# A two-layer diffusion trunk: fp32 products issued four by column group, norms spread by transposes, softmax sums by products with ones

## The chip, the cores and the metric

One core of a Trainium2 chip runs the whole program; the other cores are idle. The metric is the device time of one execution in microseconds (us), lower is better. The kernel before takes 1757.51 us, the median of three runs (1754.27 to 1760.52).

## What is computed

A trunk of two layers over 1024 latent tokens and 256 context tokens of width 1024, all in fp32. Cut to what the change touches:

```python
shift, scale, gate = jnp.split((silu_c @ ada_w[i] + ada_b[i])[:, None, :], 3, axis=-1)   # per layer, for c and c_ctx
a = modulate(rmsnorm(x, norm_g[i]), shift, scale)      # x * rsqrt(mean(x*x) + eps) * g * (1 + scale) + shift
...
# layer 0, latent attention: q, kv and the gate come out of a @ w_in
q = rmsnorm(cq, q_norm_g) @ w_uq;  kv = rmsnorm(ckv, kv_norm_g) @ w_ukv
p = jax.nn.softmax(s, axis=-1)                         # 1280 keys, 8 heads, 1024 queries
o = einsum('bhqk,bkhd->bqhd', p, v)
y = (o * silu(gate)) @ w_out
x = x + gate * y                                       # the adaLN gate
# layer 1, Hyena: two long convolutions; then the final rmsnorm
```

## The kernel before, in words

Tensors lie feature-major: 128 features on the partitions, tokens along the free axis, 512 at a time. Large products are made in three fp32r passes (`mm3`, lines 117 to 121): each operand is split into a rounded high part, copied by ScalarE (ACT, line 96), and the rest, a subtraction on VectorE (DVE, line 97). TensorE (PE) gets one 128x512 matmul for each pass. A scheduler in the tile framework sets each engine's order when the program is built; the code's order and the pools' buffers are what it starts from.

Four kinds of small product are made in plain fp32, and every one of them appears as two records in the trace, since such a matmul runs as two passes.

- **AdaLN** (`ada`, lines 133 to 162). silu(c) and silu(c_ctx) are two of 32 columns of a stationary tile `sc`. Each 512 columns of the weights give one matmul, 128x32 against 128x512, whose result lies on 32 of the 128 partitions of one bank: the group q (0 to 3) is chosen by `tile_position=(0, 32 * q)`. There are four calls: layer 0's shift and scale (four groups, pages of 512 columns, during the first 60 us), then, between the input projections of `work` (lines 570 to 584), layer 0's gate (two groups), layer 1's shift and scale (four) and layer 1's gate (two), out of two buffers `aw` of 1024 columns. Eight feature tiles make each; a matmul is issued as its columns have landed. All in all 96 matmuls.
- **Sums of squares** (`rms`, lines 345 to 375). ACT squares a tile (line 355), a matmul with a 128x32 tile of ones adds it over the partitions, again in column group k % 4 (line 356). Squares lie in three buffers of the pool `stage` in layer 0, in three of `sq` in layer 1's norm, in four at the end. Then the sums are transposed to columns (line 363), and DVE makes 1/rms of them. There are 12 such norms.
- **Spread** (`spread`, lines 377 to 383). The 1/rms column of 128 tokens, broadcast to 128 columns, is the stationary operand against the identity: an fp32 product that puts the row on every partition. Four of them fill a bank.
- **Softmax denominators** (`attend`, lines 773 to 830). The attention runs through 16 units (head, half of the queries) of 10 key tiles. For each key tile PE makes the scores S, ACT the exponentials p, DVE splits p and adds it to `acc` (line 804); PE multiplies by the values into O, two tiles later. Beside this the next unit's queries are multiplied by all keys once more for the row maxima (`row_max`, lines 724 to 739): two banks `apx`, each reduced by DVE (line 733). After a unit, in steps between the next unit's key tiles: O times the gate (line 816); four fp32 matmuls of 128 columns with ones, in the four column groups (line 821); a RECIPROCAL of 128x128 (line 823); four fp32 matmuls with `pick`, which spread the result to all partitions (line 828); and the multiplication (line 829). The bank for both comes from the pool `pj` of two, which also serves queries, keys and values.

The filters of layer 1 (`filters`, lines 268 to 342) are made in the first 440 us, interleaved with the input projections in a fixed ratio of generator steps: 120 filter steps to 60 of `work`. `ring` (line 201) is DVE work of such a step. SyncE (SP) issues nearly all loads, in one queue.

Of the kernel before, what the change touches and what calls it, by code (L numbers as in the profile page):

```python
# [11 lines left out]
F32 = mybir.dt.float32  # L12
F32R = mybir.dt.float32r
# [6 lines left out]
P = 128  # L20
# [26 lines left out]
def run(gen):  # L47
    """The value that a generator returns."""
    while True:
        try:  # L50
            next(gen)
        except StopIteration as e:
            return e.value


class Net:
# [42 lines left out]
    def feed(self, tiles, bufs=3, side=None):  # L99
        """The weights [128, K * 128] of the coming projections, in their order."""  # L100
# [4 lines left out]
    def weights(self):  # L105
        """The next piece of the weights, the one after it being loaded as well."""
# [26 lines left out]
    def ada(self, layer, part, page, bank, width=1024, queue=None):  # L133
        """part 0: shift and scale, part 1: gate."""
        nc = self.nc
        res, gs = self.adac[layer]
        ps = bank()
        nq = 2 if part else 4
        np_ = 32 * nq
        for k in range(KD):  # L140
            for s in range(0, nq * 512, width):
                w = page()
                o = 2048 * part + s
                (queue or nc.sync).dma_start(out=w, in_=self.a["adaw"][layer, k, :, o : o + width])
                for j in range(0, width, 512):
                    q = (s + j) // 512
                    nc.tensor.matmul(ps[32 * q : 32 * q + 32, :], lhsT=self.sc[:, k, :], rhs=w[:, j : j + 512],
                                     start=(k == 0), stop=(k == KD - 1), tile_position=(0, 32 * q))
            yield
        row = page()  # L150
        nc.scalar.copy(out=row[:np_, :512], in_=ps[:np_, :])
        tp = bank().rearrange("p (j c) -> p j c", j=4)
        for j in range(4):
            nc.tensor.transpose(out=tp[:, j, :np_], in_=row[:np_, j * P : (j + 1) * P], identity=self.ident[:np_, :np_])
        for r in range(2):
            c = slice(16 * part, 16 * part + 4 * nq)
            nc.vector.tensor_tensor(out=res[:, c, r].rearrange("p (q j) -> p j q", j=4), in0=tp[:, :, r:np_:32],
                                    in1=self.col(f"b{layer}", 16 * part, 4 * nq).rearrange("p (q j) -> p j q", j=4),
                                    op=ALU.add)
            if part == 0:  # L160
                nc.vector.scalar_tensor_tensor(out=gs[:, :, r], in0=res[:, 8:16, r], scalar=1.0,
                                               in1=self.col(f"g{layer}", 0, 8), op0=ALU.add, op1=ALU.mult)

# [37 lines left out]
    def ring(self, two, page, ze, zo, same):  # L201
        """Residues of 8-tile sequences ze (mod x^1024-1), zo (mod x^1024+1) in the 8 blocks."""
# [17 lines left out]
        B = [page().rearrange("p (s j c) -> p s j c", s=2, j=2) for _ in range(2)]  # [+-, j]  # L220
# [3 lines left out]
        t = page().rearrange("p (r s c) -> p r s c", r=2, s=2)  # [re/im, +-]  # L224
# [26 lines left out]
    def forward(self, two, bank, mats, i, b):  # L251
        """Spectrum of block i, [128, (re | im)] in one bank."""
# [92 lines left out]
    def rms(self, xs, n, bank, sqtile):  # L345
        """1/rms of n <= 512 tokens as columns [128, n / 128]."""
# [1056 lines left out]
```

## Time and profile before

| | |
|---|---|
| median of three runs | 1757.51 us |
| lowest, highest | 1754.27, 1760.52 us |
| span of the profiled execution, first to last instruction | 1753.2 us |
| mean granted TensorE clock | 0.995 |
| PE busy (matmul) | 1687.9 us, 96% |
| PE weight loads | 1310.8 us, 75% |
| DVE busy | 1408.3 us, 80% |
| ACT busy | 759.3 us, 43% |
| moved by DMA | 207.23 MB |

The span leaves out what lies before the first and after the last instruction; the profiled execution has no other time of its own, and its span stands 4.3 us under the median. Busy time is the union of an engine's instructions; matmuls overlap in the pipeline, so that the start-to-start distance is what one costs. A waiting time is put down to whoever released the waiting instruction last.

### The profile page before, as it was taken

Reading aid. Unit: us, or ns where it says so; the run is one execution under the profiler, and the core shown is the slowest. Engines: PE = TensorE matmul, PEld = TensorE weight load, DVE = VectorE, ACT = ScalarE, POOL = GpSimd, SP = SyncE. Lnnn points to the kernel's source line nnn. Section 1 sums busy time; section 2 is a strip of 40 time slices with the busy share of each in tenths; the row PEclk is TensorE's granted clock in tenths of the full one; section 3 lists DMA queues with packets and bytes.
Section 4 is the critical chain, followed back from the end, with each engine's and each line's share of the span. In section 5 each row is a group of like instructions: output and inputs, shape, how many; then the busy total and the mean of one; then the engine's idle time right before and its main releaser. Section 6 shows DMA issues by size and latency. Waiting matters only on the chain.

```text
span 1753.2 us, 23341 instructions
## 1 busy us (share of the span) xinstructions
PE 1687.9 (96%) x8368; PEld 1310.8 (75%) x8368; DVE 1408.3 (80%) x2528; ACT 759.3 (43%) x1315; POOL 15.1 (1%) x43
## 2 busy tenths in 40 slices
PE   7999999799999999999999999999999999999996
PEld 2367666687788888888877766888888888887874
DVE  4786978796687877887877455999999999999956
ACT  4533444435455555555555344433433343343313
POOL 1000000000000000000000010000000000000000
PEclk9999999999999999999999999999999999999999
DMA  9766666436101001010022772232332333234545
GB/s 308 249 186 193 193 199 204 138 93 194 36 27 43 19 29 40 19 32 25 19 67 79 245 249 87 84 101 88 106 114 81 104 87 111 91 118 128 188 149 209
DMA packets 139033, 207.23 MB, mean 118 GB/s; under 512 B 13386, under 2 KB 67361, under 8 KB 138788
## 3 DMA queue, kind: packets, MB, share of 16 engines
q1 hardware_dynamic: 135780, 195.05, 35.6%
q0 software_dynamic: 3136, 10.69, 1.9%
q8 instruction: 66, 1.08, 0.3%
q14 instruction: 51, 0.42, 0.1%
HBM read 149.97 MB, written 53.61 MB: 116 GB/s over the span
## 4 chain that ended last, share of the span: by engine, by line
PE 81%; DMA 9%; DVE 6%; ACT 2%; issue 1%; SPq 1%; DVEq 0%; ACTq 0%
PE pj L119 12%; PE pj L121 12%; PE pj L120 12%; PE apx L731 2%; PE S L119 2%; PE S L795 2%; PE S L120 2%; PE S L794 2%; PE S L121 2%; PE apx L732 2%; PE O L121 2%; PE O L120 2%; PE O L119 2%; PE fu L119 2%; DMA dec<-in_dec 2%; PE fy L119 2%
## 5 line engine op out<-in xcount | busy, mean ns | idle before, releaser
L96 ACT CAST w<-wr 128x512 fp32r<-128x512 f32 (+1 forms) x154 | 93.7, 609 | 276.0 <-PE pj L120 150.3
L119 PE MATMUL pj<-a,w 128*128 128x512 f32 x512 | 203.2, 397 | 1.7 <-ACT a L389 1.7
L120 PE MATMUL pj<-a,w 128*128 128x512 f32 x512 | 203.3, 397 | 0.0
L121 PE MATMUL pj<-a,w 128*128 128x512 f32 x512 | 203.1, 398 | 0.0
L797 ACT ACTIVATE p<-S 128x512 f32<-128x512 f32 x160 | 95.7, 598 | 167.6 <-PE S L795 160.7
L97 DVE TENSOR_TENSOR w<-wr,w 128x512 fp32r<-128x512 f32 (+1 forms) x154 | 102.0, 670 | 63.4 <-ACT w L96 63.0
L804 DVE TENSOR_TENSOR acc<-acc,p 128x512 f32<-128x512 f32 x144 | 99.1, 688 | 29.0 <-ACT p L797 28.6
L97 DVE TENSOR_TENSOR p<-p 128x512 fp32r<-128x512 f32 x160 | 109.7, 685 | 8.9 <-ACT p L96 8.6
L96 ACT CAST bh<-raw 128x512 fp32r<-128x512 f32 x128 | 77.1, 620 | 88.2 <-DVE raw L1043 70.3
L119 PEld LDWEIGHTS pj<-a,w 128*128 128x128 f32 x512 | 96.4, 188 | 22.9 <-ACT a L389 2.4
L120 PEld LDWEIGHTS pj<-a,w 128*128 128x128 f32 x512 | 96.5, 188 | 21.4 <-issue 1.7
L121 PEld LDWEIGHTS pj<-a,w 128*128 128x128 f32 x512 | 96.6, 189 | 18.5 <-DVE w L97 0.3
L733 DVE TENSOR_REDUCE cm<-apx 128x1 f32<-128x512 f32 (+1 forms) x192 | 108.3, 594 | 2.2 <-PE apx L732 1.5
L96 ACT CAST p<-p 128x512 fp32r<-128x512 f32 x160 | 99.4, 621 | 5.0
L121 PE MATMUL pj<-pg,w 128*128 128x512 f32 (+1 forms) x248 | 95.7, 387 | 4.2 <-DVE w L97 4.2
L119 PE MATMUL pj<-pg,w 128*128 128x512 f32 (+1 forms) x248 | 95.7, 387 | 0.6 <-ACT pg L389 0.5
L120 PE MATMUL pj<-pg,w 128*128 128x512 f32 (+1 forms) x248 | 96.3, 388 | 0.0
L97 DVE TENSOR_TENSOR bl<-raw,bh 128x512 fp32r<-128x512 f32 x128 | 84.5, 684 | 9.1 <-ACT bh L96 8.8
L119 PE MATMUL u<-bh,fm 128*128 128x256 f32 (+1 forms) x200 | 66.6, 334 | 11.1 <-ACT bh L96 10.7
L731 PE MATMUL apx<-kn,qn 128*128 128x512 f32 (+1 forms) x192 | 69.9, 369 | 2.9 <-DVE cm L733 2.8
L305 DVE TENSOR_TENSOR kk<-ph,dec 128x512 f32<-128x512 f32 x64 | 42.6, 684 | 32.9 <-DMA dec<-in_dec 20.0
L119 PE MATMUL fy<-bh,dm 128*128 128x256 f32 (+1 forms) x200 | 64.1, 320 | 2.4 <-ACT bh L96 2.4
(297 smaller groups left out, 4396.8 us busy)
## 6 DMA issues: line engine op xcount, KB each, us to landing
aw<-in_adaw SPq DMA_DIRECT2D x32, 512.0 KB, 5.0
kd<-ko SPq DMA_DIRECT2D x128, 128.0 KB, 2.0
wr<-in_hw SPq DMA_DIRECT2D x64, 256.0 KB, 2.6
kt<-kd SPq DMA_DIRECT2D x56, 256.0 KB, 2.7
wr<-in_w SPq DMA_DIRECT2D x34, 256.0 KB, 3.5
dec<-in_dec SPq DMA_DIRECT2D x64, 128.0 KB, 2.5
pg<-in_adaw SPq DMA_DIRECT2D x32, 256.0 KB, 6.1
wr<-in_wo SPq DMA_DIRECT2D x32, 256.0 KB, 3.2
```

Of the source, the lines that this page charges most:

```text
L96: self.nc.scalar.copy(out=hi, in_=raw)
L97: self.nc.vector.tensor_tensor(out=lo, in0=raw, in1=hi, op=ALU.subtract)
L119: mm(out, lhsT=w[0], rhs=x[0], start=start, stop=False)
L120: mm(out, lhsT=w[0], rhs=x[1], start=False, stop=False)
L121: mm(out, lhsT=w[1], rhs=x[0], start=False, stop=stop)
L305: nc.vector.tensor_tensor(out=kk, in0=ps, in1=dec.broadcast_to([P, 2, 2, P]), op=ALU.mult)
L731: mm(b[:, :w], lhsT=qn[0][:, c], rhs=kn[0][:, o : o + w], start=True, stop=False)
L732: mm(b[:, :w], lhsT=r1[:, c], rhs=krh[:, o : o + w], start=False, stop=True)
L733: v.tensor_reduce(out=cm[:, t, i : i + 1], in_=b[:, :w], axis=AX.X, op=ALU.max)
L794: mm(S, lhsT=krh[:, c], rhs=r1, start=False, stop=False)
L797: act.activation(out=p, in_=S, func=AF.Exp, scale=ASCALE)
L804: v.tensor_tensor(out=acc, in0=acc, in1=p, op=ALU.add)
```

## The change

1. `packed` issues up to four fp32 matmuls of different column groups directly one after the other, from the last group to the first; each is tied to the one before by `issue_after`. The first one issued is the one whose data come last.
2. `ada` takes a list of parts. Layer 0's shift and scale is as before, four groups in each feature tile; layer 1's shift and scale comes next; the gates of both layers are made together in one call of four groups. That is 24 groups of four in place of 96 matmuls issued apart, 16 of them after layer 0's shift and scale.
3. `rms` squares up to four tiles before it issues their group. In layer 0 the squares lie in the pool of 41 pages, in layer 1's norm in four buffers.
4. `spread` uses a transpose of the broadcast column in place of an fp32 product with the identity.
5. A unit's end: `acc` is split into high and low parts by ACT and DVE; two fp32r matmuls of 512 columns with a 128x128 tile of ones put the sum on every partition; the RECIPROCAL has 128x512 elements, and its result is multiplied out of SBUF. `pick` is gone. The work of line 816 is unchanged.

Nothing else changes but comments. The diff, cut:

```diff
+    def packed(self, mms):
+        nc = self.nc
+        def mm(out, w, x, start, stop, q):
+            return nc.tensor.matmul(out, lhsT=w, rhs=x, start=start, stop=stop, tile_position=(0, 32 * q))
+        prev = mm(*mms[-1], len(mms) - 1)
+        for q in range(len(mms) - 2, -1, -1):
+            with self.tc.issue_after(prev.ins), self.tc.high_priority():
+                prev = mm(*mms[q], q)
...
-    def ada(self, layer, part, page, bank, width=1024, queue=None):
+    def ada(self, parts, page, bank, width):
...
-            for s in range(0, nq * 512, width):
-                w = page()
-                o = 2048 * part + s
-                (queue or nc.sync).dma_start(out=w, in_=self.a["adaw"][layer, k, :, o : o + width])
-                for j in range(0, width, 512):
-                    q = (s + j) // 512
-                    nc.tensor.matmul(ps[32 * q : 32 * q + 32, :], lhsT=self.sc[:, k, :], rhs=w[:, j : j + 512],
-                                     start=(k == 0), stop=(k == KD - 1), tile_position=(0, 32 * q))
+            cols = []
+            for layer, first, n in parts:
+                for s in range(0, n * 512, width):
+                    wd = min(width, n * 512 - s)
+                    w = page(wd)
+                    o = 512 * first + s
+                    nc.sync.dma_start(out=w, in_=self.a["adaw"][layer, k, :, o : o + wd])
+                    cols += [w[:, j : j + 512] for j in range(0, wd, 512)]
+            self.packed([(ps[32 * q : 32 * q + 32, :], self.sc[:, k, :], w, k == 0, k == KD - 1)
+                         for q, w in enumerate(cols)])
...
-        for k, x in enumerate(xs):
-            q = k % 4
-            sq = sqtile()
-            nc.scalar.activation(out=sq[:, :n], in_=x, func=AF.Square)
-            nc.tensor.matmul(ss[32 * q : 32 * q + 32, :n], lhsT=self.ones, rhs=sq[:, :n], start=(k < 4),
-                             stop=(k + 4 >= nk), tile_position=(0, 32 * q))
+        for k0 in range(0, nk, 4):
+            group = []
+            for k in range(k0, min(k0 + 4, nk)):
+                sq = sqtile()
+                nc.scalar.activation(out=sq[:, :n], in_=xs[k], func=AF.Square)
+                q = k - k0
+                group.append((ss[32 * q : 32 * q + 32, :n], self.ones, sq[:, :n], k < 4, k + 4 >= nk))
+            self.packed(group)
...
-            self.nc.tensor.matmul(out[:, P * j : P * j + P], lhsT=r[:, j : j + 1].broadcast_to([P, P]),
-                                  rhs=self.ident, start=True, stop=True)
+            self.nc.tensor.transpose(out=out[:, P * j : P * j + P], in_=r[:, j : j + 1].broadcast_to([P, P]),
+                                     identity=self.ident)
...
-        for n, _ in enumerate(self.ada(0, 0, page, abank, 512, nc.sync)):
+        for n, _ in enumerate(self.ada([(0, 0, 4)], lambda n: page(), abank, 512)):
...
-            gen = chain(self.ada(0, 1, awt, abank), self.ada(1, 0, awt, abank), self.ada(1, 1, awt, abank))
+            gen = chain(self.ada([(1, 0, 4)], awt, abank, 1024), self.ada([(0, 4, 2), (1, 4, 2)], awt, abank, 1024))
...
+            ah, al = [tp.tile([P, 512], F32R, tag=f"p{r}", name="acc", bufs=4) for r in range(2)]
+            self.split(acc, ah, al)
+            yield
             b = bank()
-            for t in range(4):
-                c = slice(P * t, P * t + P)
-                mm(b[32 * t : 32 * t + 32, 0:P], lhsT=self.ones, rhs=acc[:, c], start=True, stop=True, tile_position=(0, 32 * t))
-            ri = tp.tile([P, P], F32, tag="ri", name="ri", bufs=1)
-            v.reciprocal(out=ri, in_=b[:, 0:P])
+            mm(b, lhsT=onesr, rhs=ah, start=True, stop=False)
+            mm(b, lhsT=onesr, rhs=al, start=False, stop=True)
+            v.reciprocal(out=acc, in_=b)
             yield
-            R = bank()
-            for t in range(4):
-                c = slice(P * t, P * t + P)
-                mm(R[:, c], lhsT=pick[:, t], rhs=ri, start=True, stop=True)
-            v.tensor_tensor(out=o, in0=o, in1=R, op=ALU.mult)
+            v.tensor_tensor(out=o, in0=o, in1=acc, op=ALU.mult)
...
-        sq = lambda: pg.tile([P, 512], F32, tag="sq", name="sq", bufs=3)
+        sq = lambda: pg.tile([P, 512], F32, tag="sq", name="sq", bufs=4)
```

How the change moves instructions, at three places. First PE between the spread of layer 0's norms and the first gate projection, at about 70 to 100 us of the trace before (`ad<-aw,sc` is adaLN, `pj<-pg,w` an input projection, `u<-bh,fm` a filter's transform). Before:

```order
93 L147 MATMUL ad<-aw,sc 32x512 x2
94 L119 MATMUL u<-bh,fm_103 128x512 x2
95 L119 MATMUL pj<-pg,w 128x512
96 L147 MATMUL ad<-aw,sc 32x512
97 L120 MATMUL pj<-pg,w 128x512
98 L121 MATMUL pj<-pg,w 128x512
99 L119 MATMUL pj<-pg,w 128x512
100 L147 MATMUL ad<-aw,sc 32x512
101 L120 MATMUL pj<-pg,w 128x512
```

Now:

```order
123 L120 MATMUL pj<-pg,w 128x512
124 L121 MATMUL pj<-pg,w 128x512
125 L119 MATMUL pj<-pg,w 128x512
126 L128 MATMUL ad<-aw,sc 32x512 x4
127 L120 MATMUL pj<-pg,w 128x512
128 L121 MATMUL pj<-pg,w 128x512
129 L119 MATMUL pj<-pg,w 128x512
```

AdaLN matmuls that stood singly or in pairs between the projections stand four together.

Second DVE around the end of a unit (`cm<-apx` are row-max reductions, `p<-p` the low part of the exponentials, `og` the unit's output). Before:

```order
657 L816 TENSOR_TENSOR og<-O,gt 128x512
658 L733 TENSOR_REDUCE cm<-apx 128x1 x2
659 L823 RECIPROCAL ri<-pj 128x128
660 L97 TENSOR_TENSOR p<-p 128x512
661 L804 TENSOR_TENSOR acc<-acc,p 128x512
662 L733 TENSOR_REDUCE cm<-apx 128x1 x2
663 L97 TENSOR_TENSOR p<-p 128x512
664 L804 TENSOR_TENSOR acc<-acc,p 128x512
665 L829 TENSOR_TENSOR og<-og,pj 128x512
```

Now:

```order
660 L749 TENSOR_REDUCE cm<-apx 128x1 x2
661 L97 TENSOR_TENSOR p<-p 128x512
662 L820 TENSOR_TENSOR acc<-acc,p 128x512
663 L97 TENSOR_TENSOR acc<-acc 128x512
664 L749 TENSOR_REDUCE cm<-apx 128x1 x2
665 L97 TENSOR_TENSOR p<-p 128x512
666 L820 TENSOR_TENSOR acc<-acc,p 128x512
667 L840 RECIPROCAL acc<-pj 128x512
668 L749 TENSOR_REDUCE cm<-apx 128x1 x2
669 L97 TENSOR_TENSOR p<-p 128x512
670 L820 TENSOR_TENSOR acc<-acc,p 128x512
671 L842 TENSOR_TENSOR og<-og,acc 128x512
```

The low part of `acc` is new (row 663), and the RECIPROCAL, now of 512 columns, stands one key tile later, with the reductions, the splits and the sums of the running unit behind it.

Third SP's queue at the start (`pg<-in_adaw` are layer 0's shift and scale, `aw<-in_adaw` the next adaLN weights, `wr<-in_w` projection weights). Before:

```order
8 L298 DMA dec<-in_dec 128x256
9 L308 DMA hbias<-in_hbias 1x2x128
10 L144 DMA pg<-in_adaw 128x512 x4
11 L298 DMA dec<-in_dec 128x256
12 L144 DMA pg<-in_adaw 128x512 x12
```

Now:

```order
8 L314 DMA dec<-in_dec 128x256
9 L324 DMA hbias<-in_hbias 1x2x128
10 L314 DMA dec<-in_dec 128x256
11 L112 DMA wr<-in_w 128x512 x2
12 L156 DMA aw<-in_adaw 128x1024 x2
13 L156 DMA pg<-in_adaw 128x512 x8
```

Two projection weights and two adaLN buffers are loaded ahead of layer 0's shift and scale.

## Rows read from the trace of the kernel before

**Rows 1.** The page's busy times, and its chain of waits by engine.

```profile
PE 1687.9 (96%) x8368; PEld 1310.8 (75%) x8368; DVE 1408.3 (80%) x2528; ACT 759.3 (43%) x1315; POOL 15.1 (1%) x43
...
PE 81%; DMA 9%; DVE 6%; ACT 2%; issue 1%; SPq 1%; DVEq 0%; ACTq 0%
```

**Rows 2.** Busy us by stretch: length, PE, PEld, DVE, ACT, POOL (instructions), clock, DMA share, GB/s.

```profile
30.00:60.00 30.00, 27.97 (x99) 9.06 (x97) 21.59 (x49) 6.36 (x11) 0.00 (x0) 1.00 0.97 336
...
60.00:300.00 240.00, 231.90 (x1176) 159.89 (x1176) 192.43 (x400) 102.30 (x189) 0.00 (x0) 1.00 0.64 191
...
200.00:240.00 40.00, 38.58 (x206) 28.93 (x205) 37.90 (x83) 15.68 (x29) 0.00 (x0) 1.00 0.70 214
...
440.00:980.00 540.00, 534.51 (x2687) 432.66 (x2686) 425.97 (x731) 281.49 (x491) 0.00 (x0) 1.00 0.13 42
...
526.00:544.00 18.00, 18.00 (x93) 14.56 (x92) 16.79 (x29) 8.45 (x15) 0.00 (x0) 1.00 0.17 55
```

**Rows 3.** AdaLN matmuls, groups of instructions: count, busy us, mean ns, idle before, releaser.

```profile
L147 PE MATMUL ad<-aw,sc 128*32 128x512 f32 x128 | 38.2, 604 | 2.6 <-DMA aw<-in_adaw 2.6
L147 PE MATMUL ad<-pg,sc 128*32 128x512 f32 x64 | 25.1, 604 | 3.2 <-DMA pg<-in_adaw 3.1
```

**Rows 4.** Timeline of PE, start and length in us: one adaLN matmul, then four, with neighbours.

```profile
73.19 1.05 PE L147 MATMUL ad<-aw,sc 128*32 128x512 f32 x2
74.17 0.50 PE L120 MATMUL pj<-pg,w 128*128 128x512 f32 x1
74.50 0.39 PE L121 MATMUL pj<-pg,w 128*128 128x512 f32 x1
...
153.05 1.06 PE L147 MATMUL ad<-aw,sc 128*32 128x512 f32 x8
154.05 0.38 PE L302 MATMUL ph<-fw,hf 128*128 128x256 f32 x1
```

**Rows 5.** Chain of waits in the first 75 us: start, length, what.

```profile
47.61 5.16 DMA pg<-in_xT
```

**Rows 6.** Sums of squares: busy us in a stretch (layer 0), and as a group (layer 1).

```profile
100.00:440.00 340.00, 7.54 (x24) 1.12 (x24) 0.98 0.59 176
...
L356 PE MATMUL nb<-sq,ones 128*32 128x512 f32 x32 | 8.6, 605 | 1.6 <-ACT sq L355 1.6
```

**Rows 7.** Spreads, and transposes of the same size, groups of instructions.

```profile
L381 PE MATMUL pj<-ident,rms 128*128 128x128 f32 x72 | 9.7, 277 | 1.7 <-DVE rms L374 1.7
L1033 PE MATMUL tr<-ident,ip 128*128 128x128 f32 x128 | 19.4, 273 | 0.0
```

**Rows 8.** Timeline of PE at a unit's end: sums (L821), spread (L828), neighbours.

```profile
528.41 0.40 PE L794 MATMUL S<-r,krh 128*128 128x512 f32 x1
528.65 0.40 PE L795 MATMUL S<-r,krl 65*128 65x512 f32 x1
528.98 0.42 PE L821 MATMUL pj<-acc,ones 128*32 128x128 f32 x8
529.34 0.39 PE L731 MATMUL apx<-kn,qn 128*128 128x256 f32 x1
...
532.00 1.05 PE L828 MATMUL pj<-ri,pick 128*128 128x128 f32 x8
532.81 0.47 PE L731 MATMUL apx<-kn,qn 128*128 128x512 f32 x1
```

**Rows 9.** Reciprocals on DVE, groups of instructions: count, busy us, mean ns.

```profile
L823 DVE RECIPROCAL ri<-pj 128x128 f32<-128x128 f32 x16 | 15.2, 950 | 0.9 <-PE pj L821 0.6
L370 DVE RECIPROCAL rms<-rms 128x4 f32<-128x4 f32 (+1 forms) x12 | 2.1, 172 | 3.9 <-ACT rms L369 3.8
```

**Rows 10.** Timeline of DVE at the same unit's end.

```profile
529.48 0.96 DVE L823 RECIPROCAL ri<-pj 128x128 f32<-128x128 f32 x1
530.38 0.69 DVE L97 TENSOR_TENSOR p<-p 128x512 fp32r<-128x512 f32 x1
530.98 0.69 DVE L804 TENSOR_TENSOR acc<-acc,p 128x512 f32<-128x512 f32 x1
```

More of the change, by code (lines that the diff above doesn't have):

```diff
@@ L149, in ada @@
             yield
-        row = page()
-        nc.scalar.copy(out=row[:np_, :512], in_=ps[:np_, :])
+        row = page(512)
+        nc.scalar.copy(out=row, in_=ps)
         tp = bank().rearrange("p (j c) -> p j c", j=4)
         for j in range(4):
[L154 to L162, printed above, removed]
+            nc.tensor.transpose(out=tp[:, j], in_=row[:, j * P : (j + 1) * P], identity=self.ident)
@@ new lines, in ada @@
+        q = 0
+        for layer, first, n in parts:
+            res, gs = self.adac[layer]
+            for r in range(2):
+                c = slice(4 * first, 4 * first + 4 * n)
+                nc.vector.tensor_tensor(out=res[:, c, r].rearrange("p (q j) -> p j q", j=4),
+                                        in0=tp[:, :, 32 * q + r : 32 * (q + n) : 32],
+                                        in1=self.col(f"b{layer}", 4 * first, 4 * n).rearrange("p (q j) -> p j q", j=4),
+                                        op=ALU.add)
+                if first == 0:
+                    nc.vector.scalar_tensor_tensor(out=gs[:, :, r], in0=res[:, 8:16, r], scalar=1.0,
+                                                   in1=self.col(f"g{layer}", 0, 8), op0=ALU.add, op1=ALU.mult)
+            q += n
@@ L429, in layer0_in @@
         st = lambda: stp.tile([P, 512], F32, tag="st", name="st")
-        awt = lambda: stp.tile([P, 1024], F32, tag="aw", name="aw", bufs=2)
+        awt = lambda n: stp.tile([P, 1024], F32, tag="aw", name="aw", bufs=2)[:, :n]
         bank = lambda: ps.tile([P, 512], F32, tag="pj", name="pj", bufs=3)
@@ L454, in layer0_in @@
         load_x(0)
-        rx = [self.rms(x[0], 512, bank, st)]
+        rx = [self.rms(x[0], 512, bank, page)]
         filt.send(x[0][7])
-        for n, _ in enumerate(self.ada(0, 0, page, abank, 512, nc.sync)):
+        for n, _ in enumerate(self.ada([(0, 0, 4)], lambda n: page(), abank, 512)):
             next(filt)
@@ L460, in layer0_in @@
                 load_x(1)
-                rx.append(self.rms(x[1], 512, bank, st))
+                rx.append(self.rms(x[1], 512, bank, page))
         load_c()
         xcs = [xc[k // 2][:, LC * (k % 2) : LC * (k % 2) + LC] for k in range(KD)]
-        rc = self.rms(xcs, LC, bank, st)
+        rc = self.rms(xcs, LC, bank, page)
         ax = []
@@ L596, in layer0_in @@
             w = c.stop - c.start
-            raws.append((awt() if w > 512 else page())[:, :w])
+            raws.append(awt(w) if w > 512 else page()[:, :w])
             nc.sync.dma_start(out=raws[-1], in_=a["watt"][0][:, c])
@@ L661, in attention @@
         act.copy(out=identr, in_=self.ident)
-        pick = tp.tile([P, 4, P], F32, name="pick", bufs=1)
-        v.memset(pick, 0.0)
-        for t in range(4):
-            v.memset(pick[32 * t : 32 * t + 1, t], 1.0)
+        onesr = tp.tile([P, P], F32R, name="onesr", bufs=1)
+        act.copy(out=onesr, in_=self.one.broadcast_to([P, P]))
         ksegs = [(0, 512), (512, 512), (1024, 256)]
@@ L817, in attend @@
             yield
+            ah, al = [tp.tile([P, 512], F32R, tag=f"p{r}", name="acc", bufs=4) for r in range(2)]
+            self.split(acc, ah, al)
+            yield
             b = bank()
-            for t in range(4):
-                c = slice(P * t, P * t + P)
-                mm(b[32 * t : 32 * t + 32, 0:P], lhsT=self.ones, rhs=acc[:, c], start=True, stop=True, tile_position=(0, 32 * t))
-            ri = tp.tile([P, P], F32, tag="ri", name="ri", bufs=1)
-            v.reciprocal(out=ri, in_=b[:, 0:P])
-            yield
-            R = bank()
-            for t in range(4):
-                c = slice(P * t, P * t + P)
-                mm(R[:, c], lhsT=pick[:, t], rhs=ri, start=True, stop=True)
-            v.tensor_tensor(out=o, in0=o, in1=R, op=ALU.mult)
+            mm(b, lhsT=onesr, rhs=ah, start=True, stop=False)
+            mm(b, lhsT=onesr, rhs=al, start=False, stop=True)
+            v.reciprocal(out=acc, in_=b)
+            yield
+            v.tensor_tensor(out=o, in0=o, in1=acc, op=ALU.mult)
             nc.sync.dma_start(out=self.og_d[h, :, sl], in_=o)
```

3 lines of the change are left out of this document (removed).

## The prediction

> **What bounds the kernel now.** I read the busy times first, then the chain of waits, then the busy times by stretch. PE is busy for 96% of the span and holds 81% of the chain that ended last [rows 1]: what shortens PE's queue shortens the kernel, as long as no other engine has to be waited for. The stretches say where that may fail. Up to 60 us the DMA engines are nearly full (0.97) and PE has room. From 60 to 300 us PE is busy for 231.90 of 240 us, DVE for 192.43, and in a burst of the filter work (200 to 240 us) DVE for 37.90 of 40. In attention PE is busy for 534.51 of 540 us and DVE for 425.97 (79%); but at a unit's end and just after it (526 to 544 us) DVE is busy for 16.79 of 18 us [rows 2]. So PE binds nearly everywhere, with DVE close behind it in two places.
>
> **AdaLN after the first 60 us.** The 64 matmuls of layer 0's gate and of layer 1 are 128 records, busy for 38.2 us, with 2.6 us of waits for their weights in front of them [rows 3]. One alone, two records, keeps PE from 73.19 to 74.17; four together, eight records, from 153.05 to 154.05. The matmul behind the single one then takes 0.33 us (74.17 to 74.50) [rows 4], where two of this kind stand 0.24 us apart otherwise [rows 8]. A place in the queue thus costs about 1.1 us whether one matmul stands there or four. 38.2 / 1.05 gives 36 such places; the change leaves 16. That removes 20 x 1.1 = 22 us of PE. It isn't all gained: in 60 to 300 us DVE's 192.43 us would stand in 240 - 22 = 218 us, 88%, and the bursts at 95% are already as short as DVE lets them be. I take 18 us; the bounds are 25 us (22 and the waits) and 0.
>
> The Trainium skill (TensorEngine Tiling (Array Packing), Theoretical Speedup) gives up to four times the speed for outputs of at most 32 columns. By it these 38.2 us would fall to 9.6 and the term would be 28.6. The rows decide otherwise, since many of the 36 places hold two to four matmuls already.
>
> **The first 60 us.** Layer 0's shift and scale is busy for 25.1 us, and what it saves there is hidden by the loads of the same weights: idle time before it is put down to them [rows 3], and the DMA engines are full [rows 2]. SP now issues two `wr` of 256 KB and two `aw` of 512 KB ahead of these weights, 1.5 MB. At the 336 GB/s of this stretch [rows 2] that is 4.7 us by which the second half of x, loaded from 47.61 us on [rows 5], may be late. Against it, the `wr` and `aw` need not be loaded later, and the squares' sums of the second half and of the context (singles now) become four groups, behind which the first spread waits. I take -2 us, between +4.7 and -6.
>
> **Norms.** From 100 to 440 us the sums are busy for 7.54 us; the five norms there become five groups, four of 1.05 us and one half as wide of 0.6: 7.54 - 4.8 = 2.7 us less. In layer 1's norm 8.6 us become four groups, 4.2, and one wait of 1.6 us for a square may stay or go [rows 6]. Together 7.1 us; I take 6, because each group now waits for its last square; bounds 3 and 8.7. In the last norms the four squares of the second half are made by ACT one after the other, and the group starts with the last: the end doesn't move, 0 (a lost cover here would show as at most the 1 us of one more group).
>
> **Spreads.** Four products take 9.7 / 9 = 1.08 us, four transposes of the same size 19.4 / 32 = 0.61 [rows 7]. Ten such blocks and two half ones gain 11 x 0.47 = 5.2 us of PE; two of the ten stand where DVE or the DMA sets the pace: I take 4, bounds 2 and 5.2. About 0.5 of it lies at the very end.
>
> **A unit's end, PE.** The four sums cost 0.36 us (528.98 to 529.34); the matmul before them takes 0.33 us where 0.24 is usual (528.65 to 528.98), and the one behind about as much more, 0.55 in all. The spread costs 0.81 (532.00 to 532.81) [rows 8]. In their place stand two fp32r matmuls of 0.24. PE gains 0.55 + 0.81 - 0.48 = 0.88 us a unit, 14.1 us in 16.
>
> **A unit's end, DVE.** A RECIPROCAL of 4 columns takes 172 ns (a mean with two of 2 columns), one of 128 takes 950 [rows 9]: 6.3 ns an element. 384 more elements are 2.4 us. The low part of `acc` costs what a split costs, 0.60 us from start to start (530.38 to 530.98) [rows 10]. So DVE gets 3.0 us more a unit, 48 us in 16, and 474 of 540 - 14 = 526 us, 90%, on the whole. In a stretch as 526 to 544 us it would need 16.79 + 3.0 = 19.8 us, while PE needs 18 - 0.9 = 17.1: there PE would wait, and a unit becomes 1.8 us longer, not 0.9 shorter. Behind the long RECIPROCAL stand the running unit's reductions and splits; for them wait the two `apx` banks and the products with the values. ACT's copy of `acc` has room. Between -0.88 us a unit (no wait) and +1.8 (DVE's pace everywhere) I take -0.2, since 90% on the whole is nearer to the first while half a unit is as dense as the second: -3 us; bounds -14 and +29.
>
> On the RECIPROCAL the Trainium skill (VectorE: DVE Perf Modes, First, the fixed hardware budget) says that it divides iteratively with a repeat count of 8. At 8 cycles of 0.96 GHz an element this would make 4.3 us of 512 columns, 0.9 more than my 3.3, and 14 us more in the sum if PE waited for all of it. The trace disagrees: 128 elements would take 1067 ns by it, and take 950 [rows 9].
>
> **Sum.** 18 + 2 + 6 + 4 + 3 = 33 us less. The profiled span is 1753.2 us, 4.3 under the median of 1757.5; against the median, where the 4.3 stay, the forecast is 1757.5 - 33 = 1724.5, said as **1724 us**.
>
> **Rivals.**
> - *PE never waits in attention.* The scheduler's order puts enough scores and value products behind the RECIPROCAL; then the whole 14 us are gained, 1724.5 - 11 = 1713. For it speaks DVE's room of 10% on the whole, against it 526 to 544 us.
> - *The filters set the pace.* If DVE's chain holds 60 to 300 us, AdaLN's 18 us and half of the norms' gain go: 1724.5 + 18 + 2 = 1744. For it speaks 37.90 of 40, against it that PE is busy for 97% of the whole stretch.
> - *The long RECIPROCAL makes DVE the bound of attention.* At +1.8 us a unit: 1724.5 + 3 + 29 = 1756, no change. If PE makes no use at all of its relief, because each unit's wait falls between the same two `apx` banks, all 3.0 us count: +48 instead of -3, 1775, slower. It decides the sign from about 2.2 us a unit on. For it speaks the dense stretch; against it, that DVE idles for a fifth of attention.
> - *The groups don't share.* If four matmuls issued from the last column group to the first ran one after the other, a place would cost 4 x 0.9 us or more: 16 places 58 us against 38.2 + 2.6, nine norm groups 32 against 18, so +31 in place of -24: 1780. The rows show groups that share [rows 4], but not in which order their columns stand.
>
> **How the numbers follow.** What can be told from no change is about 0.3%, 5 us: 1752 to 1763. Forecast 0.48; no wait in attention 0.20; filters set the pace 0.20 (0.02 of it so near that it counts as the same); DVE bounds attention 0.09 (0.04 the same, 0.05 slower); no sharing 0.03, slower. Faster 0.48 + 0.20 + 0.18 = 0.86, same 0.06, slower 0.08. The forecast's own bounds are some 12 us on either side; the range of 8 in 10 takes in the first two rivals with their own spread: 1700 to 1748.
>
> **What would show it.** AdaLN after 60 us: 16 places with about 17 us busy, eight records within 1.1 us. Sums of squares in layer 1: 4.2 us. The span from 60 to 300 us now should hold the same projections some 18 us earlier. RECIPROCAL of 128x512: 3.3 us, sixteen times; DVE in attention near 90%; PE idle in attention 12 to 25 us, its waits put down to DVE on `apx`, scores or value products. I am wrong if the RECIPROCAL takes over 4 us, if PE idles for more than 30 us in attention, or if the filters' end doesn't move.

## The result, and the profile after

The changed kernel takes 1741.63 us (median of four runs, 1735.72 to 1743.25) against 1755.89 us for the kernel before on the same chip: a ratio of 0.9917, with a 95% interval of 0.9892 to 0.9941. That is 14 us less, where 33 were forecast. In a later set of runs (e13 below) it was 1739.15 against 1753.84 us, a ratio of 0.9922 (0.9903 to 0.9941). The profiled execution is the fastest of the four (1735.72 us), with a span of 1733.9 us.

The busy times by engine, and the chain by engine [rows 1]:

```profile
PE 1635.3 (94%) x8096; PEld 1300.2 (75%) x8096; DVE 1442.4 (83%) x2539; ACT 766.1 (44%) x1331; POOL 15.4 (1%) x43
...
PE 79%; DMA 8%; DVE 8%; ACT 3%; issue 1%; SPq 1%; DVEq 0%; ACTq 0%
```

PE is busy for 53 us less, but the span is only 19.3 us shorter: PE is now idle for 6% of it instead of 4%. The stretches say where [rows 2]:

```profile
0.00:60.00 60.00, 36.78 (x144) 13.83 (x144) 33.77 (x71) 23.00 (x37) 5.76 (x20) 0.80 1.00 344
60.00:300.00 240.00, 213.24 (x1165) 162.82 (x1165) 190.84 (x405) 104.63 (x192) 0.00 (x0) 0.95 0.62 190
300.00:440.00 140.00, 126.86 (x650) 104.00 (x651) 106.38 (x220) 63.28 (x116) 3.69 (x7) 0.95 0.49 145
440.00:980.00 540.00, 532.12 (x2497) 428.57 (x2496) 469.19 (x757) 291.06 (x512) 0.00 (x0) 1.00 0.15 48
```

From 60 to 300 us PE is now busy for 213 of 240 us (231.90 before), at a mean granted clock of 0.95 (1.00 before). In attention it is as full as before. The window from 440 to 980 us takes in more of layer 1 than before, so DVE is read in attention alone: it goes from 414.7 of 516.7 us (80%) to 450.4 of 504.6 (89%).

```profile
450.30:967.00 516.70, 511.64 (x2577) 414.19 (x2579) 414.70 (x715) 273.04 (x475) 0.00 (x0) 1.00 0.11 35
...
446.50:951.10 504.60, 500.33 (x2364) 403.37 (x2363) 450.42 (x732) 280.00 (x492) 0.00 (x0) 1.00 0.11 36
```

The groups that the change rewrote, which answer to [rows 3, 6, 7]: AdaLN after and in the first 60 us, sums of squares from 100 to 440 us (`st`) and in layer 1 (`nb`), and layer 1's spreads:

```profile
L128 PE MATMUL ad<-aw,sc 128*32 128x512 f32 x128 | 17.9, 633 | 8.0 <-DMA aw<-in_adaw 8.0
L128 PE MATMUL ad<-pg,sc 128*32 128x512 f32 x64 | 12.7, 881 | 8.4 <-DMA pg<-in_adaw 8.3
L128 PE MATMUL pj<-st,ones 128*32 128x512 f32 (+1 forms) x24 | 4.8, 569 | 0.0
L128 PE MATMUL nb<-sq,ones 128*32 128x512 f32 x32 | 4.3, 605 | 0.4 <-ACT sq L372 0.4
L399 PE MATMUL nb<-ident,rms 128*128 128x128 f32 x8 | 1.2, 279 | 0.0
```

The four products of a group do run side by side. Eight records start at 150.90 us, and the next matmul at 151.89:

```profile
150.90 1.06 PE L128 MATMUL ad<-aw,sc 128*32 128x512 f32 x8
151.89 0.50 PE L121 MATMUL pj<-pg,w 128*128 128x512 f32 x1
```

Busy times fell as forecast: AdaLN from 38.2 to 17.9 us, layer 1's sums from 8.6 to 4.3. But PE's wait for AdaLN's weights rose from 2.6 to 8.0 us.

At the end of an attention unit, the timeline of DVE [rows 10] has the low part of `acc`, the long RECIPROCAL, and the next unit's reductions right behind it:

```profile
527.26 0.69 DVE L97 TENSOR_TENSOR acc<-acc 128x512 fp32r<-128x512 f32 x1
529.99 3.35 DVE L840 RECIPROCAL acc<-pj 128x512 f32<-128x512 f32 x1
533.26 0.96 DVE L749 TENSOR_REDUCE cm<-apx 128x1 f32<-128x512 f32 x2
```

All RECIPROCALs of this kind as a group [rows 9]:

```profile
L840 DVE RECIPROCAL acc<-pj 128x512 f32<-128x512 f32 x16 | 53.6, 3351 | 0.0
```

And PE's waits from 446 to 951 us, that is in all of attention (us in total, times, longest):

```profile
PE apx L747 <- DVE cm L749: 1.9, 6, 0.7
PE S L119 <- ACT p L813: 1.0, 3, 0.3
PE pj L754 <- DVE mx L751: 0.7, 1, 0.7
PE po L121 <- DVE w L97: 0.3, 1, 0.3
```

The RECIPROCAL takes 3.35 us, sixteen times, and in 505 us PE waits for DVE for less than 3. Nor does PE stand still while a RECIPROCAL runs, or in the stretch that the prediction took as the dense one [rows 2], where DVE is busy for 17.81 of 18 us:

```profile
529.99:533.34 3.35, 3.35 (x16) 2.72 (x15) 3.35 (x3) 1.22 (x2) 0.00 (x0) 1.00 0.00 0
526.00:544.00 18.00, 18.00 (x86) 14.76 (x85) 17.81 (x29) 8.46 (x16) 0.00 (x0) 1.00 0.08 29
```

**A ledger of two stretches.** The table splits the time of PE between the first projection and the first scores. "Waits" are the gaps between matmuls. "Clock" is what matmuls lost while the granted clock stood at 1.2 instead of 2.4 GHz: the step from start to start less the median step of the same kind at 2.4 GHz. "Work" is the rest. "Attention" is from the first scores to the last unit's last product. All of it is from profiled executions, one of each kernel, and how work and clock are split holds to about 1 us. They aren't medians: those of the changed kernel and of e15 are 6 and 5 us under their kernel's median, that of e8 is 4 over. In the profile of e14, which is e8's kernel again, the first scores come at 435.2 us, so rows that differ by a few us tell nothing.

| kernel | first projection | work | waits | clock | first scores | attention |
|---|---|---|---|---|---|---|
| before | 72.9 | 351.4 | 22.6 | 3.4 | 450.3 | 516.6 |
| changed | 78.1 | 316.3 | 38.5 | 13.7 | 446.5 | 504.6 |
| e3, changed without packed AdaLN | 81.5 | 339.4 | 21.9 | 6.1 | 448.9 | 504.9 |
| e4, most AdaLN loads left out | 79.6 | 314.5 | 24.8 | 11.9 | 430.9 | 505.3 |
| e8, halved groups | 78.1 | 321.0 | 29.3 | 11.9 | 440.3 | 506.1 |
| e15, halved and spaced | 78.1 | 319.8 | 24.7 | 7.2 | 429.8 | 505.0 |

Attention is 12 us shorter, from layer 1's norm to the mixer's first matmul (967.0 to 1104.3 us before, 951.1 to 1084.1 now) it is 4 us less, and the mixer is unchanged. But the first scores come only 4 us earlier, though PE has 35 us less work between the two marks. Waits took back 16, the clock 10 and the later start 5. That start is no loss by itself: 50 matmuls of the filters' transforms (`u`) stand ahead of the first projection where 20 stood before, some 5 us of work at their usual distance. So the work saved is nearer 30 us than 35.

### The profile page after: what moved, and what is told of

Read it like the earlier page. It is cut to its first block, busy times and chain, and to the rows that moved or that the text cites. A ratio compares the mean times of both kernels' runs of the same rounds, so it can differ in the third digit from the quotient of the medians.

```text
span 1733.9 us, 22766 instructions
## 1 busy us (share of the span) xinstructions
PE 1635.3 (94%) x8096; PEld 1300.2 (75%) x8096; DVE 1442.4 (83%) x2539; ACT 766.1 (44%) x1331; POOL 15.4 (1%) x43
## 4 chain that ended last, share of the span: by engine, by line
PE 79%; DMA 8%; DVE 8%; ACT 3%; issue 1%; SPq 1%; DVEq 0%; ACTq 0%
PE pj L121 13%; PE pj L119 13%; PE pj L120 12%; PE O L120 2%; PE S L119 2%; PE O L119 2%; PE S L811 2%; DMA kd<-ko 2%; PE O L121 2%; PE apx L747 2%; PE S L810 2%; PE S L121 2%; PE S L120 2%; PE apx L748 2%; DMA aw<-in_adaw 2%; PE fu L119 2%
## 5 line engine op out<-in xcount | busy, mean ns | idle before, releaser
L121 PE MATMUL pj<-pg,w 128*128 128x512 f32 (+1 forms) x248 | 98.0, 395 | 9.5 <-DVE w L97 9.5
L119 PE MATMUL pj<-pg,w 128*128 128x512 f32 (+1 forms) x248 | 96.7, 393 | 2.4 <-ACT pg L407 2.4
L120 PE MATMUL pj<-pg,w 128*128 128x512 f32 (+1 forms) x248 | 98.1, 396 | 0.6 <-DVE pg L408 0.6
L748 PE MATMUL apx<-krh,r 128*128 128x512 f32 (+1 forms) x192 | 67.2, 358 | 0.0
```

The source lines that it names most:

```text
L119: mm(out, lhsT=w[0], rhs=x[0], start=start, stop=False)
L120: mm(out, lhsT=w[0], rhs=x[1], start=False, stop=False)
L121: mm(out, lhsT=w[1], rhs=x[0], start=False, stop=stop)
L748: mm(b[:, :w], lhsT=r1[:, c], rhs=krh[:, o : o + w], start=False, stop=True)
```

## The experiments

Ratios are to the kernel before, on the same chip.

**Which part gives what.** e1 is the kernel before with the softmax part alone, e2 with the packed AdaLN alone, e3 the changed kernel with `ada` as before.

> The kernel before with the softmax part of the change alone (sums by two fp32r products, reciprocal of 128x512). Theory P, paid back: attention keeps all of its gain and the first 440 us give back what AdaLN and the norms save. Then this part alone gives most of the whole: the first scores start at 450 us as before, the last value product ends at about 955 (967 before), and the time is 10 to 14 us under the kernel before. Rival R, reciprocal: DVE takes back most of it; then 0 to 5 us under the kernel before.

> The kernel before with AdaLN in groups of four alone. Theory P: PE is less busy up to 440 us, waits for loads and filters and runs at the lower clock for more than 20 us, so the first scores start between 446 and 454 us (450.3 before) and the time stays within 4 us of the kernel before. Rival Q, PE binds there as the prediction had it: the first scores at 430 to 435 us, 15 to 20 us faster.

> The changed kernel with AdaLN as it was before. Theory P: the 22 us of PE work come back between waits, the clock stays at its upper level for longer, and the time is within 4 us of the changed kernel (1742). Rival Q: 15 to 20 us slower than the changed kernel, so no faster than the kernel before.

e1: 1743.66 us (1742.21 to 1747.53), ratio 0.9942 (0.9922 to 0.9962). e2: 1758.04 (1754.31 to 1762.98), 1.0021 (1.0008 to 1.0034). e3: 1740.14 (1734.49 to 1741.63), 0.9912 (0.9890 to 0.9935). Theory P holds in all three. Against 1754.74 us before, the softmax part alone gives 11 us, norms and spreads together some 3.5 more (e1 to e3; the intervals overlap), and the packed AdaLN nothing: it costs 3 us alone, and leaves the changed kernel where it is without it. Yet it takes 23 us of work off PE (339.4 to 316.3).

**What eats AdaLN's gain.** e4 leaves out 14 of the 16 pairs of loads of the three later vectors.

```diff
-                    w = page(wd)
-                    nc.sync.dma_start(out=w, in_=self.a["adaw"][layer, k, :, o : o + wd])
+                    if width == 512 or k == 0:
+                        w = page(wd)
+                        nc.sync.dma_start(out=w, in_=self.a["adaw"][layer, k, :, o : o + wd])
+                        kept[layer, s] = w
+                    else:
+                        w = kept[layer, s]
```

> The changed kernel, in which three of the four AdaLN vectors use the weights of the first feature tile for all eight, so that 14 of 16 pairs of loads are left out and no group waits for its loads; PE's work is the same. If the waits for the two weight buffers (8 us up to 440 us in the changed kernel) and the lower clock behind them are what pays the gain back, the first scores start at 432 to 438 us (446.5 in the changed kernel) and the time is 8 to 14 us under it. Rival, the filters' chain on DVE sets the pace: first scores within 3 us of 446.5, time within 3 us of the changed kernel.

1723.13 us (1720.34 to 1725.01), ratio 0.9820 (0.9802 to 0.9838). That is more than was expected. With the filters and all of PE's work in place, leaving out the loads makes the kernel 18 us faster: they hold this stretch back. That these are the very 18 us forecast for AdaLN isn't shown, since the same loads were not left out of a kernel with AdaLN as before (e3), which might gain as well. The clock isn't the main cause, since 11.9 us are lost to it here too.

Where the loads bite was looked for in the waits between 78 and 260 us. Before, for PE and DVE:

```profile
PE ad L147 <- DMA aw<-in_adaw: 2.3, 4, 1.3
...
DVE kk L305 <- DMA dec<-in_dec: 9.9, 8, 2.5
```

in the changed kernel:

```profile
PE ad L128 <- DMA aw<-in_adaw: 8.0, 7, 1.7
PE ph L318 <- DVE rms L392: 3.3, 1, 3.3
...
DVE kk L321 <- DMA dec<-in_dec: 12.4, 4, 5.7
DVE w L97 <- ACT w L96: 7.9, 1, 7.9
```

and in e3, the changed kernel with AdaLN as before:

```profile
PE ad L159 <- DMA aw<-in_adaw: 4.4, 5, 1.5
...
DVE kk L317 <- DMA dec<-in_dec: 14.5, 7, 5.6
DVE w L97 <- ACT w L96: 9.0, 3, 7.4
```

In the changed kernel PE's own wait is 5.7 us more than before, and the filters' chain on DVE stands once for 5.7 us on its `dec` load (2.5 before) and once for 7.9 on projection weights. These loads are in SP's queue too. But e3 has both long waits of DVE as well (5.6 and 7.4), so packing AdaLN isn't what makes them. Only PE's own wait is longer with it (8.0 against 4.4). The DMA issues from 78 to 150 us count the AdaLN loads (the number behind x, KB each, median us to landing where enough of them show it); before:

```profile
aw<-in_adaw SPq DMA_DIRECT2D x12, 512.0 KB, 3.6
```

and in the changed kernel:

```profile
aw<-in_adaw SPq DMA_DIRECT2D x18, 512.0 KB
```

Each of the first twelve places now asks for 1 MB, into both buffers of `aw`. SP isn't held longer by it: its waits at the line that issues the AdaLN loads add up to 29 us between 78 and 300 us, against 37 before and 30 in e3.

**The start.** e5 issues the context's loads right behind those of x (`load_c()` moved up behind `load_x(1)`).

> The changed kernel with the four loads of the context tokens issued on SP right behind those of x instead of behind the filters' first writes. In the changed kernel they were issued at 65.4 us (before: 52.9) and the first spread came at 75.4 us (before: 69.4). Theory S (the start is late because of these loads): the first spread comes at 66 to 70 us and the kernel ends 4 to 8 us before the changed one (1734 to 1738 us at 1741.6 for it). Rival T (the start is late because TensorE ran its first 24 us at the 1.2 GHz level and because of the squares): the first spread stays at 73 to 76 us and the time within 2 us of the changed kernel's.

1739.05 us (1737.71 to 1745.77), 0.9921 (0.9894 to 0.9947). The first spread came at 73.6 us instead of 75.4, and the time is that of the changed kernel: theory S falls. Rival T's reason isn't shown by this. Its "first 24 us" are, in the changed kernel's trace, 23.9 us at 1.2 GHz in three pieces between 23.7 and 57.8 us.

**SP's queue, or the buffers.** e6 issues these loads on POOL, e7 spreads the groups over more places, e8 halves the groups.

```diff
# e6
-                    nc.sync.dma_start(out=w, in_=self.a["adaw"][layer, k, :, o : o + wd])
+                    (nc.sync if width == 512 else nc.gpsimd).dma_start(out=w, in_=...)
# e7, in work(): one loop for all projections
+            every = chain(gates(range(0, 3)), latent_kv(), gates(range(3, 5)), context(), gates(range(5, 6)))
+            for m, _ in enumerate(every):
+                if m % 5 in (0, 2):
+                    next(gen, None)
+                yield
# e8: the same loop with next(gen) at each place, and in ada
+        for e in range(512 // half):
+            for k in range(KD):
...
+                        w = page(1024).rearrange("p (q c) -> p q c", q=4) if w is None else w
+                        nc.sync.dma_start(out=w[:, i : i + n], in_=src[:, :, half * e : half * e + half])
```

> The changed kernel with the loads of three of the four AdaLN vectors issued by POOL's queue instead of SP's; buffers, groups and places as in the changed kernel. The run without most of these loads showed that they hold up the first 440 us by some 18 us. Theory V (SP's queue: an AdaLN load that waits for its buffer holds the filters' loads and writes and the projections' weights that are queued behind it): first scores at 432 to 438 us instead of 446.5, total 8 to 15 us under the changed kernel's. Rival W (the buffers: a group needs both, so its 1 MB can't be under way while the group before it is in hand, whatever queue issues it): TensorE's waits on these loads stay at 6 to 10 us, first scores at 443 to 447 us, total within 4 us of the changed kernel's.

> The changed kernel with its 16 groups of 1 MB spread over the 46 places of the projections (two of every five) instead of taking each of the first twelve and six more. Theory W (two buffers for one group of 1 MB, used again 6 us later): with some 16 us between groups the loads land before their group, TensorE's waits on them fall from 8 us to under 2, first scores at 434 to 441 us, total 6 to 13 us under the changed kernel's. Theory V (SP's queue held by loads that wait for their buffers) expects as much at most half: fewer, longer spaced waits still hold SP, total 2 to 6 us under. If neither counts (the clock or the filters decide) the time stays within 2 us.

> The changed kernel with each group cut into two of 256 columns: one 512 KB buffer holds all four operands of a group, so that the other buffer's load runs ahead of it, with the 32 groups and their ends at 34 of the 46 places. Theory W: TensorE's waits on these loads under 2 us, groups of some 0.6 us, together 2 us more than 16 groups of 1.05; first scores at 434 to 441 us; total 6 to 13 us under the changed kernel's. Theory V: waits of SP on a buffer stay, 2 to 6 us under. A rival against both: rows of 1 KB in the loads cost the DMA engines more and the time rises by 0 to 5 us.

e6: 1757.27 us (1750.45 to 1761.80), 1.0019 (1.0004 to 1.0034). Worse than either theory said: PE's waits on these loads doubled, and POOL's queue itself stood still for buffers:

```profile
PE ad L128 <- DMA aw<-in_adaw: 15.7, 9, 3.3
...
POOL aw L156 <- PE ad L128: 187.9, 15, 47.1
```

So freeing SP of them was no gain, and theory V falls in this form; why it cost 16 us was not followed up. e7: 1740.32 us (1739.13 to 1742.21), 0.9921 (0.9902 to 0.9941), no gain either: the groups were spread, and PE still waited for their loads for 9.6 us between 60 and 440 us, once for 4.8. By the code, both of a group's buffers come free at once and are filled one behind the other. e8: 1732.53 us (1729.03 to 1736.62), 0.9877 (0.9849 to 0.9905), inside theory W's range, though its wait (5.6 us) isn't under 2. e8 also takes other places than the changed kernel; e7 shows that other places alone bring nothing.

**What PE's work is worth there.** e9 multiplies each of the 16 groups twice (the sum is halved on its way out).

```diff
+            for i in range(twice):
+                self.packed([(..., k == 0 and i == 0, k == KD - 1 and i == twice - 1) for q, w in enumerate(cols)])
```

> The changed kernel with the 16 later AdaLN groups each multiplied twice and the sum halved when it is copied out: same loads, same buffers, 16 more groups of some 1.05 us (16.8 us) on TensorE. Theory X (TensorE's own work still sets the length of the stretch from the first projection to the first scores, and its waits lie on top): the stretch grows from 368.4 us by 12 to 17 us and the total to 1753 to 1759. Rival Y (the filters' chain on VectorE or the loads set the length, TensorE's work fits into its waits): the stretch grows by under 5 us, total 1741 to 1746; the granted clock's losses fall from 13.7 us, since TensorE has fewer gaps.

1749.84 us (1746.09 to 1759.27), 0.9969 (0.9951 to 0.9986): 8 to 11 us over the changed kernel for 16 us of work, between X and Y. The profiled execution is its slowest (1759.27); in it the stretch grows by 12.7 us and the waits fall by under 2. So PE's work still counts there for half or more, but not in full.

**The start's norms.** e10 is e8 with the three norms of the start in the form of before; e11 is e10 with AdaLN's 34 steps at three of every four places (`if m % 4 in (0, 1, 2)`).

> The kernel with the halved groups (first projection at 78.1 us, 1732.5 us) with the three norms of the start as before the change: squares in the three stage buffers, one matmul behind each square, not fours with squares in pages. Theory Z (at the start the packed norm is what loses: its first matmul waits for the fourth square, and the squares' pages hold what is loaded behind them): the first projection comes at 72 to 75 us, total 1727 to 1730. Rival (the later start comes from TensorE's lower granted clock there, which the packed first AdaLN vector brings): the first projection stays at 77 to 80 us, total 1731 to 1735.

> As the run with the halved groups and the start's norms of before, with the 34 AdaLN steps at three of every four of the 46 places instead of at the first 34. Theory W (two buffers, refilled every 6 us): TensorE's waits on these loads fall from 5.6 us to under 3, total 2 to 4 us under that run's. Rival (a place later only moves the wait, as the run with groups spread by fives showed): within 2 us of it.

e10: 1742.36 us (1740.19 to 1746.44), 0.9928 (0.9902 to 0.9955). The first projection comes at 74.0 us, as theory Z has it, but the first scores at 447.0, later than e8's 440.3. The earlier mark was in part work put off (work behind it grew from 321.0 to 325.2 us), and Z falls. The rest of the 10 us by which e10 is slower than e8 isn't explained. e11: 1735.13 (1731.06 to 1740.84), 0.9887 (0.9855 to 0.9919), 7 us better by the medians, though the two intervals overlap. Its traced waits on the loads are longer than e10's (9.1 to 7.1 us), but the traces can't explain the step: e11's is of its slowest execution, and the two spans are 1739.0 and 1739.4 us.

**Dependence or traffic, and a better version.** e12 is e8 with all loads issued, while every product takes the first buffer's weights. e13 is the changed kernel, e14 is e8, e15 is e8 at three of every four places, these three in five rounds.

```diff
# e12
-                        w = page(1024).rearrange("p (q c) -> p q c", q=4) if w is None else w
+                        if w is None:
+                            t = page(1024).rearrange("p (q c) -> p q c", q=4)
+                            if k + e == 0:
+                                kept = t
+                            w = kept
# e15, against e8
-                if m % 1 in (0,):
+                if m % 4 in (0, 1, 2):
```

> The kernel with the halved groups (1732.5 us), with every load of the three later AdaLN vectors still issued, but their products taken with the first loaded buffer's weights each time: 14 of 16 weights of each half are loaded and never multiplied. Theory W (the loss is TensorE's groups waiting for their loads): waits on these loads gone, total 1722 to 1727 us, as where the loads were left out (1723.1). Rival V2 (the loss is the traffic: 12 MB in SP's queue and on the DMA engines ahead of the filters' and projections' loads): total 1730 to 1735 us, the same as the halved groups.

> The changed kernel again, beside the halved groups on one chip: 1739 to 1744 us.

> The halved groups again: 1730 to 1735 us, 6 to 11 us under the changed kernel, if that run was no accident of its chip; within 3 us of the changed kernel if it was.

> The halved groups with their 34 steps at three of every four of the 46 places. If the spacing helped by itself where it was tried with the start's norms of before (7 us), 1726 to 1732 us here; if that was the order that the scheduler happened to give, within 4 us of the halved groups at the first 34 places.

| run | us | ratio |
|---|---|---|
| e12 | 1737.13 (1731.78 to 1738.49) | 0.9908 (0.9890 to 0.9925) |
| e13, changed kernel | 1739.15 (1736.22 to 1744.75) | 0.9922 (0.9903 to 0.9941) |
| e14, halved | 1728.95 (1727.22 to 1735.97) | 0.9867 (0.9848 to 0.9885) |
| e15, halved and spaced | 1726.66 (1721.39 to 1730.16) | 0.9843 (0.9823 to 0.9862) |

e12 takes PE's dependence on the loads away, and is 8 us slower than e14, above what either theory said. So PE's own wait for them isn't what decides; with the loads still issued, the gain of leaving them out isn't there. Why it is slower than e14 stays open. But the traffic isn't a bound either: e15 issues the same loads, 32 of 512 KB or 16 MB (not 12, as the expectation has it), and is at 1726.66 us, 3.5 over e4 (on another chip), which issued almost none. So what counts is how and when they are issued, not that they are. e14 confirms e8: 10 us under the changed kernel beside it. e15 is another 2.3 us under e14, but their intervals overlap and both branches of its expectation hold, so that the spacing helps by itself isn't shown. From 78 to 150 us e15 issues 9 of them, the changed kernel 18:

```profile
aw<-in_adaw SPq DMA_DIRECT2D x9, 512.0 KB
```

That number alone doesn't decide: e7 issues 10 there and gains nothing, e14 issues 12. Nor do SP's waits ahead of them, 34 us in e15 against 29. From 60 to 450 us e15's PE waits for little, except once on a filter block:

```profile
PE u L119 <- ACT bh L96: 9.0, 3, 8.7
PE ad L128 <- DMA aw<-in_adaw: 3.9, 6, 0.9
PE pj L121 <- DVE w L97: 3.6, 3, 1.7
```

And its stretch from 60 to 300 us:

```profile
60.00:300.00 240.00, 218.93 (x1329) 166.64 (x1329) 203.42 (x423) 109.17 (x200) 0.00 (x0) 0.96 0.66 197
```

DVE does 203 us of work in that stretch, against 191 in the changed kernel (205 in e4): the filters run ahead. Their last transform ends at 396.7 us in e15 and at 395.3 in e4, against 407.6 in the changed kernel and 412.9 before. e15 beats both kernels, by 27 us against the one before and by 12.5 against the changed one, and their intervals don't touch.

## Why the prediction was half right

The direction was right and the time lies in the range, but the forecast of 33 us was more than twice the 14 measured. AdaLN and the start together gave 20 less than forecast, norms and spreads some 6 less; attention gave 8 more and hid part of it.

- **AdaLN after the first 60 us, 18 us: this step failed.** Its arithmetic on PE held: 16 places and 17.9 us busy, 23 us of work gone. But e2 and e3 put its worth at nothing (between 3 us lost and 0). The step took PE's relief for time and named DVE's bursts as the only limit; the loads of this stretch it put at nothing but 2.6 us of waits. The runs show them in its place: with most AdaLN loads left out and PE's work the same, the first scores come at 430.9 us instead of 446.5 (e4), and with the same loads cut in halves the kernel is 10 us faster (e14). With the packed groups, PE's saved time went into waits (17 us) and the lower clock (8), by the ledger's rows of e3 and the changed kernel. How the loads hold the stretch stays open. That it is the 1 MB at once, 18 loads from 78 to 150 us where there were 12, fits e8 and e14, but e7, e12 and the waits of e3 don't decide for it. The term's lower bound, 0, was right for another reason than the one given.
- **The rival "the filters set the pace"** has almost the measured time (1744) but not the mechanism. e15 and e4 bring 12 to 18 us back without touching the filters' work on DVE, so DVE's arithmetic wasn't what held that stretch. That the times agree is luck: attention gave 8 us more than that rival has, the other terms less. The range held because it took this rival in.
- **Attention, 3 us: mis-sized.** Prices were right: RECIPROCAL 3.35 us (3.3 forecast), DVE busy for 89% of attention (90%). The choice of -0.2 us a unit between -0.88 and +1.8 was wrong: e1 measured 11 us, 0.7 a unit, and the rival "PE never waits in attention" is what happened. I took the dense stretch for half of a unit and let PE wait there; in the rows after, DVE is busy for 17.81 of its 18 us, and PE has scores and value products in hand for all 18. In all of attention PE waits for 4 us, where 12 to 25 were expected.
- **Norms 6 and spreads 4.** Their work left PE as forecast: 8.6 to 4.3 us in layer 1 and 7.54 to 4.8 before; layer 1's norm with its neighbours is 4 us shorter. In the first stretch of e3 there are 12 us less work (351.4 to 339.4), of which some 5 are filter work that now stands ahead of the first projection (57 matmuls of the transforms instead of 20); yet the first scores moved only from 450.3 to 448.9. e1 to e3 gives 3.5 us for both, less than the 10 forecast. Part of it may be what e9 shows, that PE's work doesn't count there in full; why the first projection comes later than the moved work explains (72.9 to 81.5) e10 didn't settle.
- **The first 60 us, 2 us.** The first spread came 6 us later. e5 and e10 moved such marks earlier without moving the end with them.
- **The signs of being wrong** didn't catch the failed step. RECIPROCAL and PE's idle time in attention stayed under their limits, and the filters' end (their last transform, 412.9 to 407.6 us) did move, by 5 us. The sign should have asked how far.

Two estimates of the prediction come from the Trainium skill. Its factor of up to four (TensorEngine Tiling (Array Packing), Theoretical Speedup), taken in full, would have made 9.6 us of 38.2; measured were 17.9. Its repeat count of 8 for the RECIPROCAL (VectorE: DVE Perf Modes, First, the fixed hardware budget), read as 8 cycles an element, would have made 4.3 us; measured were 3.35.

What stays open: by which way the loads hold the stretch; what e3 would gain from leaving them out, or from AdaLN steps spread over all places; and how much of e11 over e10 is the spacing, since the order that the scheduler gives can change with such an edit. Whether the time lost to the lower clock could be won back wasn't tried.

## What to carry to other kernels

When work on the busiest engine is packed into fewer places, don't take the work saved for time: ask what else the stretch needs, and what each place now needs at once. Fewer and bigger groups ask for bigger loads, and with as many buffers as one group takes, none of them can run ahead. Here it paid to cut the group so that one buffer holds all of its operands (e8 and e14, 10 us); spreading the groups over more places as well brought 2 more, within the noise (e15). And where an engine is at 79% on the whole, read how much of its dense stretch other engines can run past before taking half of the worst case.

## What had not been expected of the hardware

- Where PE had less to do, it also got a slower clock. In the first 60 us of the kernel before, PE was busy for 49.77 us at the full 2.4 GHz:

```profile
0.00:60.00 60.00, 49.77 (x155) 14.48 (x155) 32.85 (x73) 24.19 (x39) 5.56 (x20) 1.00 0.96 325
```

  In the changed kernel it was busy for 36.78 there, at a mean granted clock of 0.80: 23.9 of the 60 us stood at 1.2 GHz, and an AdaLN record took 881 ns instead of 604. In e3 it was busy for 43.94 us, and the clock was 1.00. The clock isn't fixed by the kernel: in e13, the changed kernel again, it was 0.86 at 36.76 us. From 260 to 300 us of the changed kernel, with PE busy for 30.64 of 40 us, the clock was 0.91:

```profile
260.00:300.00 40.00, 30.64 (x176) 26.55 (x175) 35.44 (x76) 17.59 (x35) 0.00 (x0) 0.91 0.39 115
```

- The clock cost the changed kernel 13.7 us of PE time before the first scores, against 3.4 before. e15 lost 7.2 and e4 11.9, with nearly the same waits (24.7 and 24.8), so the waits alone don't set it.
- Loads of 1 KB rows (e8) landed no later than those of 4 KB rows (e7): the DMA issues from 78 to 150 us show a median of 4.7 us for 512 KB in both. The rival of e8's expectation falls by this.
